# Attention of two heads at a time: rotary products on the two halves of the rows, values per tile

## The chip, the cores and the metric

The kernel runs on one core of a Trainium2 chip. The metric is the time of one execution in microseconds on the device; the median of three runs is given.

## What is computed

The reference is one layer of a diffusion backbone over 512 latent tokens and 256 context tokens, width 1024. After a modulated norm and one input projection, latent attention (4 heads) and a matrix memory (mLSTM, 4 heads) work side by side; their outputs are joined, projected and added; then a product-key retrieval of experts follows. The part that matters here is the attention. A head has 128 channels without and 64 channels with a rotary position, and reads 768 keys (256 context, 512 latent):

```
def attend(q, k, v):
    s = jnp.einsum('bhqd,bhkd->bhqk', q, k).astype(jnp.float32) * (MLA_QK ** -0.5)
    p = jax.nn.softmax(s, axis=-1).astype(v.dtype)
    return jnp.einsum('bhqk,bhkd->bhqd', p, v)
...
mla_lat, mla_ctx = mla_mixer(cols_lat[..., :MLA_COLS], ..., rope, not last)
ml_lat, ml_ctx = mlstm_mixer(cols_lat[..., MLA_COLS:], ...)
x = x + gt1 * (jnp.concatenate([mla_lat, ml_lat], axis=-1) @ w_out[l])
h2 = rmsnorm(x, g_norm2[l]) * (1.0 + sc2) + sh2
x = x + gt2 * peer(h2, w_pq[l], sub_keys[l], expert_u[l], expert_v[l])
```

Everything is float32.

## The kernel before

Tokens are cut into tiles of 128: tiles 0 to 3 are the latents. Tiles 1 to 3 go through the dense path, tile 0 goes a way of its own later on. The order of stages is: modulation and input projection; keys, values and queries; mLSTM together with the attention of tiles 1 to 3; output projection (`w_out`); the norm and the query projection of the retrieval (`w_pq`), with the sixteen best of each key half on VectorE; then `first()` and `second()`, which rank on VectorE while tile 0 is brought through and the first expert blocks are multiplied; then a long loop over 128 expert blocks (lines 1384 to 1412).

`attention(tiles, store, nm)` (line 837) is a generator. For each head and each tile it makes the scores (lines 846 and 847: for 512 and then 256 keys a product over 128 rows for the channels without position and a product over 64 rows for the rotary ones, accumulated in the same place), takes the maximum on VectorE (849), its scaled negative (850), the exponential with its sum on ScalarE (852), normalises on VectorE (853, 854), transposes the six blocks on PE (858) and copies them to `pt` on ScalarE (859). After the last tile of a head come six products with the values over all tiles of the call (864, 384 columns for three tiles), and `store` brings the result away. The queries and keys of the rotary part lie two heads in a column block: an even head on rows 0 to 63, an odd one on rows 64 to 127 (`es`). On PE each of these float32 products shows in the trace as two weight loads and two matmuls.

`split` (218, 219) writes a rounded copy on ScalarE and the rest, by subtraction, on VectorE or GpSimd. `mm3` (255 to 257) makes the three products of such pairs.

Score tiles come from a pool of two slots of 1024 columns (`wide`, tag s); from line 1029 on that pool has one slot. Results of products with the values come from a pool `jbank` of two slots, which the mLSTM steps (785, 787) use too; transposes use `bank`. `mlstm()` (736) is a generator over two pairs of heads.

`weave` draws from several generators in proportion, so that their instructions alternate in the program:

```
    weave((queries((1, 2, 3, 0)), 4), (islice(ml, CFG["w"][0]), CFG["w"][1]))
    weave((ml, CFG["w"][2]), (attention((1, 2, 3), lambda h, p_: split(ch[:, h], cl[:, h], p_), "D"), 13))
```

Tile 0 (`att0`, line 902) takes its first two steps before the norm that follows the output projection (`CFG["a"]` is (0, 2)), and the rest inside `tile0_x` (1092), after the pools have been changed. Outside the first stage and the expert loop the order on each engine is set by a planner, which takes the ready instruction that comes first in the program. `PLACE` is a list of places, one for each buffer in the order in which buffers are taken.

Of the kernel before, what the change touches and what calls it, by code (L numbers as in the profile page):

```python
# [17 lines left out]
AF = mybir.ActivationFunctionType  # L18
OP = mybir.AluOpType
AX = mybir.AxisListType  # L20
P = 128
D = 1024
# [27 lines left out]
ENDED = object()  # L50
CFG = dict(nv=2, r=8, l=(0, 34, 124), pre=28, f=(17, 7, 7, 27, 2, 4), oa=2, og=2, gt=2, a=(0, 2), ps=(('g', 2), ('j', 1), ('b', 2), ('s', 1)), w=(22, 22, 22), ko=(4, 5, 6, 7, 0, 1, 2, 3), m=(5, 7, 4, 7, 4, 4, 1), ne=lambda v, g: g, sc=lambda k, n: n == 256 or k % 2, wq=lambda nc: nc.sync, we=lambda i, v, g: g)

# [49 lines left out]
class Ring:  # L102
# [5 lines left out]
    def next(self):  # L108
        self.i += 1
        return self.v[(self.i - 1) % len(self.v)]  # L110
# [5 lines left out]
def weave(*parts):  # L116

    parts = [[g, n, 0] for g, n in parts]
    while parts:
        x = min(parts, key=lambda x: x[2] / x[1])  # L120
        x[2] += 1
        if next(x[0], ENDED) is ENDED:
            parts.remove(x)


def body(ctx, tc, nc, x_t, ctx_t, cc, w_ada_t, w_ada_n, w_in, w_uq, w_ukv, w_out, w_pq, keys_t,
         exp_u, exp_v, exp_ut, pcol, prow, pcon, rope_c, rope_s, jmat, rst, dsel, dmask, out, dbg=None):
    dbg = dbg or {}
    V, A, G, T = nc.vector, nc.scalar, nc.gpsimd, nc.tensor
# [8 lines left out]
    ar = Arena(PLACE, lambda: nc.n_instructions())  # L138
# [13 lines left out]
    start = ExitStack()  # L152
# [7 lines left out]
    def bank():  # L160
        return ps["b"].tile([P, 512], F32, name="b")

    def jbank():
        return ps["j"].tile([P, 512], F32, name="j")

    def wide():
        return ps["s"].tile([P, 1024], F32, name="s")
# [22 lines left out]
    ident = ar.take("ident", [P])  # L190
# [10 lines left out]
    small = ar.ring("small", 16, [4])  # L201
# [15 lines left out]
    def split(hi, lo, src, eng=V):  # L217
        A.activation(hi, src, AF.Copy)  # L218
        eng.tensor_tensor(lo, src, f32(hi), op=OP.subtract)  # L219
# [68 lines left out]
    with tc.manual_schedule():  # L288
# [11 lines left out]
        for j, row in enumerate((s_l, s_x)):  # L300
            for h in range(2):
                p_ = bank() if h else jbank()
# [43 lines left out]
        p_, tots = jbank(), []  # L346
# [22 lines left out]
        p_ = wide()  # L369
# [235 lines left out]
    knT, krT = ar.take("knT", [4, NT]), ar.take("krT", [2, NT])  # L605
    vm = ar.take("vm", [6, 4, P])
    knr, krpr = ar.ring("kn", 2, [4, P]), ar.ring("krp", 2, [2, 2, 64])
    for t in range(6):
        o = slice(t * P, (t + 1) * P)
        p_ = wide()  # L610
# [84 lines left out]
    def q_of(i):  # L695
        return (qn0, qr0, slice(0, P)) if i == 0 else (qnD, qrD, slice((i - 1) * P, i * P))
# [138 lines left out]
    scale = 192.0 ** -0.5  # L835

    def attention(tiles, store, nm):
        n = len(tiles) * P
        pt, ppr = ar.take("pt" + nm, [6, n]), ar.ring("pp" + nm, 2, [768])
        for h in range(4):  # L840
            es = slice((h % 2) * 64, (h % 2) * 64 + 64)
            for j, i in enumerate(tiles):
                qn, qr, o = q_of(i)
                p_ = wide()
                for c0, c1 in ((0, 512), (512, 768)):
                    T.matmul(p_[:, c0:c1], qn[:, h, o], knT[:, h, c0:c1], start=True, stop=False)  # L846
                    T.matmul(p_[:, c0:c1], qr[es, h // 2, o], krT[es, h // 2, c0:c1], start=False, stop=True)  # L847
                mx = small.next()
                V.tensor_reduce(mx[:, 0:1], p_[:, :768], axis=AX.X, op=OP.max)
                V.tensor_scalar(mx[:, 0:1], mx[:, 0:1], -scale, None, op0=OP.mult)  # L850
                pp = ppr.next()
                A.activation(pp, p_[:, :768], AF.Exp, bias=mx[:, 0:1], scale=scale, accum_out=mx[:, 1:2])
                V.reciprocal(mx[:, 1:2], mx[:, 1:2])
                V.tensor_scalar(pp, pp, mx[:, 1:2], None, op0=OP.mult)
                for t3 in range(2):
                    p_ = bank()
                    for t in range(3):
                        T.transpose(p_[:, t * P:(t + 1) * P], pp[:, (3 * t3 + t) * P:(3 * t3 + t + 1) * P], ident)
                    A.activation(pt[:, 3 * t3:3 * t3 + 3, j * P:(j + 1) * P],
                                 p_[:, :384].rearrange("p (t q) -> p t q", t=3), AF.Copy)  # L860
                if j == len(tiles) - 1:
                    p_ = jbank()[:, :n]
                    for t in range(6):
                        T.matmul(p_, vm[:, t, h], pt[:, t], start=(t == 0), stop=(t == 5))
                    store(h, p_)
                yield
        ppr.give()
        ar.give("pt" + nm)


    ch, cl = ar.take("ch", [KD, 384], F32R), ar.take("cl", [KD, 384], F32R)
    ml = mlstm()
    weave((queries((1, 2, 3, 0)), 4), (islice(ml, CFG["w"][0]), CFG["w"][1]))
    weave((ml, CFG["w"][2]), (attention((1, 2, 3), lambda h, p_: split(ch[:, h], cl[:, h], p_), "D"), 13))
    xT = ar.take("xD", [KD, 384])
    nc.sync.dma_start(xT, x_t[:, :, P:])
    for h in range(4):
        p_ = bank()
# [3 lines left out]
    p_ = bank()  # L882
# [6 lines left out]
    for wg in range(4):  # L889
        wh, wl = wpull()  # L890
        for c2 in range(2):
            k2 = 2 * wg + c2
            cs = slice(c2 * P, c2 * P + P)
            p_ = jbank()[:, :384]
# [4 lines left out]
    r2, hx = ar.take("r2", [384]), ar.ring("hx", 3, [384])  # L899

    cat0 = ar.take("cat0", [4, P])
    att0 = attention((0,), lambda h, p_: A.activation(cat0[:, h], p_, AF.Copy), "G")
    for _ in range(CFG["a"][0]):
        next(att0)
    rms_bcast(r2, hx, xT, 384)
# [2 lines left out]
    for k in range(KD):  # L908
        t = hx.next()
# [94 lines left out]
    for wg in range(8):  # L1004
# [3 lines left out]
        for c2 in range(2):  # L1008
            cs = slice(c2 * P, c2 * P + P)
            p_ = jbank()[:, :384]  # L1010
            mm3(p_, [(wh[:, k, cs], wl[:, k, cs], hi[:, k], lo[:, k]) for k in range(KD)])
            A.activation(qT[:, c2], p_, AF.Copy)
        p_ = wide()
# [408 lines left out]
    for g in range(3):  # L1422
        for half in range(2):
            d_, t = slice(half * 512, half * 512 + 512), tmr.next()
# [85 lines left out]
```

## Time and profile before

| | us |
|---|---|
| median of 3 runs | 1732.3 |
| lowest and highest | 1725.78, 1736.87 |
| profiled execution | 1736.11 |
| its span | 1734.3 |
| PE busy | 1629.1 |
| VectorE busy | 1332.7 |
| ScalarE busy | 735.3 |
| GpSimd busy | 443.6 |

The profile comes from one execution; the mean granted clock of TensorE in it is 0.975 of 2.4 GHz. PE stands for matmuls, PEld for weight loads, DVE for VectorE, ACT for ScalarE, POOL for GpSimd, SP for the queue that issues most DMAs. In a row of instructions, `s` is the score pool, `j` and `b` are the other pools of products, `sp` is on-chip memory. Start times are counted from the start of the span.

### The profile page before, as it was taken

The page shows a single profiled execution, that of the slowest core. Times are in us where ns is not written, and L with a number is a line of the kernel's source. Part 1 is how long each engine was busy: PE and PEld are TensorE (multiplying, and loading weights), DVE is VectorE, ACT ScalarE, POOL GpSimd, SP SyncE. Part 2 cuts the span into 40 slices and gives each one's busy share as a digit, 9 for nine tenths or more (in the row PEclk, how much of TensorE's full clock was granted, in tenths as well). Part 3 has the DMA queues.
Part 4 walks back from the last instruction along what each step waited for, and adds up shares of the span by engine and source line. Part 5 has one row for each costly group of instructions (what it writes and reads, how often), then busy time and mean ns, then how long its engine had stood idle before and what let it go on. Part 6 is the DMA issues. An engine that isn't in the chain of part 4 may idle for free.

```text
span 1734.3 us, 25190 instructions
## 1 busy us (share of the span) xinstructions
PE 1629.1 (94%) x9119; PEld 1412.4 (81%) x9119; DVE 1332.7 (77%) x2857; ACT 735.3 (42%) x1404; POOL 443.6 (26%) x339
## 2 busy tenths in 40 slices
PE   6889999998988999969899999999999999999988
PEld 4669854588968989857689999999999999999977
DVE  6896165556899997958876887888888888888874
ACT  4563544434345545534353433333333333334322
POOL 6621400033400000000101333333333434444311
PEclk8999988999999999989999999999999999999989
DMA  8456301133314757565777999999999999999962
GB/s 340 145 184 218 104 25 37 31 110 122 119 50 170 267 214 256 204 202 162 260 237 214 341 321 335 336 328 322 325 339 322 318 343 331 323 335 334 314 226 82
DMA packets 155244, 400.92 MB, mean 231 GB/s; under 512 B 13424, under 2 KB 70192, under 8 KB 150000
## 3 DMA queue, kind: packets, MB, share of 16 engines
q1 hardware_dynamic: 108320, 232.05, 39.0%
q0 software_dynamic: 36864, 134.23, 22.5%
q10 hardware_dynamic: 9936, 33.03, 4.9%
q8 instruction: 71, 1.16, 0.3%
q14 instruction: 53, 0.43, 0.1%
HBM read 367.28 MB, written 31.99 MB: 230 GB/s over the span
## 4 chain that ended last, share of the span: by engine, by line
PE 72%; DVE 17%; ACT 4%; DMA 4%; issue 2%; POOL 0%; ACTq 0%; SPq 0%; DVEq 0%
PE o L1283 27%; PE u L255 9%; PE u L257 9%; PE u L256 9%; PE j L255 2%; PE j L256 2%; PE j L257 2%; DVE sp L219 2%; PE s L846 1%; DVE sp L1186 1%; PE s L847 1%; PE g L1196 1%; ACT sp L218 1%; DMA sp<-in_exp_ut 1%; DMA sp<-in_w_ada_t 1%
## 5 line engine op out<-in xcount | busy, mean ns | idle before, releaser
L218 ACT ACTIVATE sp<-sp 128x512 fp32r<-128x512 f32 (+2 forms) x674 | 406.4, 637 | 465.5 <-PE u L256 257.5
L1283 PE MATMUL o<-sp 128*128 128x512 f32 x2304 | 550.1, 393 | 21.1 <-ACT sp L218 14.9
L219 DVE TENSOR_TENSOR sp<-sp,sp 128x512 fp32r<-128x512 f32 (+1 forms) x650 | 407.6, 658 | 158.7 <-ACT sp L218 158.6
L1283 PEld LDWEIGHTS o<-sp 128*128 128x128 f32 x2304 | 432.1, 189 | 113.4 <-ACT sp L218 15.8
L255 PE MATMUL u<-sp,sp 128*128 128x384 f32 x1024 | 349.2, 341 | 14.1 <-ACT sp L1269 7.8
L257 PE MATMUL u<-sp,sp 128*128 128x384 f32 x1024 | 347.8, 340 | 6.7 <-DVE sp L219 6.7
L256 PE MATMUL u<-sp,sp 128*128 128x384 f32 x1024 | 346.1, 338 | 0.0
L1347 POOL DMA_INDIRECT sp<-in_exp_u,sp x128 | 137.2, 1072 | 679.2 <-PE o L1283 360.0
L255 PEld LDWEIGHTS u<-sp,sp 128*128 128x128 f32 x1024 | 194.0, 189 | 20.9 <-ACT sp L1074 8.4
L1347 POOL DMA_INDIRECT sp<-in_exp_v,sp x128 | 151.9, 1187 | 222.3 <-DVE sp L1323 204.9
L257 PEld LDWEIGHTS u<-sp,sp 128*128 128x128 f32 x1024 | 193.7, 189 | 9.0 <-DVE sp L219 7.9
L256 PEld LDWEIGHTS u<-sp,sp 128*128 128x128 f32 x1024 | 193.8, 189 | 3.9
L219 POOL TENSOR_TENSOR sp<-sp,sp 128x2048 fp32r<-128x2048 f32 (+1 forms) x24 | 96.5, 4024 | 264.6 <-ACT sp L218 264.6
L1323 DVE SCALAR_TENSOR_TENSOR sp<-sp 128x1024 f32<-128x1024 f32 x127 | 162.5, 1279 | 0.2
L1311 DVE CUSTOM_DVE_ANT_0 sp<-sp 128x1024 f32<-128x1024 f32 x128 | 155.6, 1215 | 0.0
L257 PE MATMUL j<-sp,sp 128*128 128x256 f32 (+2 forms) x448 | 140.7, 314 | 5.0 <-DVE sp L398 5.0
L255 PE MATMUL j<-sp,sp 128*128 128x256 f32 (+2 forms) x448 | 143.0, 321 | 1.7 <-ACT sp L218 0.9
L256 PE MATMUL j<-sp,sp 128*128 128x256 f32 (+2 forms) x448 | 141.0, 315 | 0.0
L1269 ACT ACTIVATE sp<-u 128x384 f32<-128x384 f32 x100 | 49.2, 492 | 173.4 <-PE u L257 160.5
L1271 DVE TENSOR_TENSOR sp<-sp,sp 128x384 f32<-128x384 f32 x107 | 61.2, 572 | 63.2 <-ACT sp L1269 46.3
L257 PEld LDWEIGHTS j<-sp,sp 128*128 128x128 f32 x448 | 84.6, 189 | 7.5 <-DVE sp L398 5.7
L255 PEld LDWEIGHTS j<-sp,sp 128*128 128x128 f32 x448 | 84.8, 190 | 6.0 <-issue 1.7
(343 smaller groups left out, 1804.3 us busy)
## 6 DMA issues: line engine op xcount, KB each, us to landing
sp<-in_exp_ut SPq DMA_DIRECT2D x128, 512.0 KB, 5.4
sp<-in_exp_v SPq DMA_DIRECT2D x128, 512.0 KB, 6.3
gd<-sp ACTq DMA_DIRECT2D x48, 512.0 KB, 4.5
sp<-gd SPq DMA_DIRECT2D x32, 768.0 KB, 9.7
sp<-in_w_ada_t SPq DMA_DIRECT2D x38, 512.0 KB, 4.4
sp<-in_w_pq SPq DMA_DIRECT2D x16, 1024.0 KB, 5.1
sp<-in_w_in SPq DMA_DIRECT2D x8, 1024.0 KB, 5.2
sp<-in_w_out SPq DMA_DIRECT2D x8, 1024.0 KB, 4.8
```

Source lines behind the costliest of these rows:

```text
L218: A.activation(hi, src, AF.Copy)
L219: eng.tensor_tensor(lo, src, f32(hi), op=OP.subtract)
L255: T.matmul(ps, lh, rh, start=(first and i == 0), stop=False)
L256: T.matmul(ps, lh, rl, start=False, stop=False)
L257: T.matmul(ps, ll, rh, start=False, stop=(last and i == n - 1))
L846: T.matmul(p_[:, c0:c1], qn[:, h, o], knT[:, h, c0:c1], start=True, stop=False)
L1269: A.activation(ge, pu.pop(c_), AF.Gelu)
L1271: V.tensor_tensor(blk(w), blk(ge), gts[c_ // 4][:, :, c_ % 4], op=OP.mult)
L1283: T.matmul(ob[2 * g + half], l_[:, g * P:g * P + P], fl(r_), start=(c_ == 0 and i == 0), stop=(c_ == P - 1 and i == 2))
L1311: V.tensor_tensor_reduce(out=u, in0=u, in1=h2t, scale=1.0, scalar=0.0, op0=OP.mult, op1=OP.add, accum_out=act[:, j:j + 1])
L1323: V.scalar_tensor_tensor(acc, v, act[:, j:j + 1], acc, op0=OP.mult, op1=OP.add)
L1347: G.indirect_dma_start(out=r_, out_offset=None, in_=table, in_offset=bass.IndirectOffsetOnAxis(ap=col, axis=0))
```

## The change

Attention goes by pairs of heads. For each pair and each tile both heads' score tiles are taken, the two products without position are made one behind the other, then the two rotary products, of which one works on rows 0 to 63 and one on rows 64 to 127; then softmax, transposes, copies and the product with the values follow for each head, for this tile alone (128 columns). `pt` becomes a ring of two buffers of 128 columns, `store` is called for each head and tile, and the places of some buffers change. The number of steps that the generator gives to `weave` stays.

```
-        n = len(tiles) * P
-        pt, ppr = ar.take("pt" + nm, [6, n]), ar.ring("pp" + nm, 2, [768])
-        for h in range(4):
-            es = slice((h % 2) * 64, (h % 2) * 64 + 64)
+        ptr, ppr = ar.ring("pt" + nm, 2, [6, P]), ar.ring("pp" + nm, 2, [768])
+        for pair in range(2):
             for j, i in enumerate(tiles):
                 qn, qr, o = q_of(i)
-                p_ = wide()
+                S = [wide(), wide()]
                 for c0, c1 in ((0, 512), (512, 768)):
-                    T.matmul(p_[:, c0:c1], qn[:, h, o], knT[:, h, c0:c1], start=True, stop=False)
-                    T.matmul(p_[:, c0:c1], qr[es, h // 2, o], krT[es, h // 2, c0:c1], start=False, stop=True)
+                    for e in range(2):
+                        T.matmul(S[e][:, c0:c1], qn[:, 2 * pair + e, o], knT[:, 2 * pair + e, c0:c1], start=True, stop=False)
+                    for e in range(2):
+                        es = slice(e * 64, e * 64 + 64)
+                        T.matmul(S[e][:, c0:c1], qr[es, pair, o], krT[es, pair, c0:c1], start=False, stop=True)
...
+                for e in range(2):
+                    h, p_, mx = 2 * pair + e, S[e], small.next()
...
+                    pp, pt = ppr.next(), ptr.next()
...
+                        A.activation(pt[:, 3 * t3:3 * t3 + 3], p_[:, :384].rearrange("p (t q) -> p t q", t=3), AF.Copy)
+                    p_ = jbank()[:, :P]
                     for t in range(6):
                         T.matmul(p_, vm[:, t, h], pt[:, t], start=(t == 0), stop=(t == 5))
-                    store(h, p_)
-                yield
+                    store(h, j, p_)
+                    yield
...
-    weave((ml, CFG["w"][2]), (attention((1, 2, 3), lambda h, p_: split(ch[:, h], cl[:, h], p_), "D"), 13))
+    weave((ml, CFG["w"][2]), (attention((1, 2, 3), lambda h, j, p_: split(ch[:, h, j * P:j * P + P], cl[:, h, j * P:j * P + P], p_), "D"), 13))
```

## Rows read from the trace of the kernel before

**Rows 1.** The page: busy us of each engine, share of the span, instructions.
```profile
PE 1629.1 (94%) x9119; PEld 1412.4 (81%) x9119; DVE 1332.7 (77%) x2857; ACT 735.3 (42%) x1404; POOL 443.6 (26%) x339
```
**Rows 2.** Table of stretches: length, busy us by engine, granted clock, DMA, GB/s.
```profile
285.00:300.00 15.00, 14.97 (x78) 8.86 (x76) 5.83 (x17) 5.22 (x13) 0.00 (x0) 1.00 0.00 0
...
315.00:330.00 15.00, 15.00 (x61) 7.46 (x60) 9.48 (x21) 5.73 (x14) 0.00 (x0) 1.00 0.04 10
...
440.00:500.00 60.00, 53.77 (x304) 49.78 (x302) 57.62 (x346) 16.89 (x26) 13.75 (x3) 0.97 0.29 93
...
900.00:1734.00 834.00, 819.35 (x4124) 745.10 (x4122) 657.34 (x987) 315.94 (x590) 285.76 (x251) 0.99 0.87 304
```
**Rows 3.** Timeline, 250 to 300 us: start, us, engine, line, idle time before.
```profile
260.00 0.70 PE L847 MATMUL s<-sp,sp 64*128 64x256 f32 x2
...
261.51 0.95 DVE L849 TENSOR_REDUCE sp<-s 128x1 f32<-128x768 f32 x1
...
266.33 2.07 PE L846 MATMUL s<-sp,sp 128*128 128x512 f32 x2 [0.86 <-ACT sp L852]
```
**Rows 4.** Table of stretches of 5 us after the first scores.
```profile
260.00:265.00 5.00, 1.82 (x10) 1.25 (x10) 5.00 (x10) 2.54 (x4) 2.00 (x4) 0.96 0.59 210
265.00:270.00 5.00, 4.14 (x7) 1.07 (x5) 4.27 (x7) 3.44 (x11) 1.02 (x2) 0.50 0.16 41
...
275.00:280.00 5.00, 5.00 (x15) 2.69 (x16) 2.97 (x8) 3.59 (x10) 0.00 (x0) 0.67 0.00 0
```
**Rows 5.** Chain of waits in order of time, 200 to 360 us.
```profile
300.03 1.05 PE s L846 x2
301.09 1.05 PE s L847 x2
302.14 0.63 PE s L846 x2
302.77 0.63 PE s L847 x2
...
304.45 0.66 PE b L858 x6
305.11 1.05 PE s L847 x2
...
352.05 0.43 PE s L846 x2
352.49 0.53 PE j L255 x2
```
**Rows 6.** The same chain: products with the values of one head.
```profile
306.16 4.07 PE j L864 x12
```
**Rows 7.** Timeline of PE, 319.6 to 321.2 us.
```profile
319.72 0.69 PE L847 MATMUL s<-sp,sp 64*128 64x512 f32 x1
319.80 0.49 PE L785 MATMUL j<-sp,sp 64*128 64x129 f32 x2
320.25 0.59 PE L847 MATMUL s<-sp,sp 64*128 64x512 f32 x1
320.77 0.70 PE L846 MATMUL s<-sp,sp 128*128 128x256 f32 x2
```
**Rows 8.** Chain of waits, 352 to 560 us: tile 0's output projection.
```profile
525.29 2.05 PE j L1101 x16
...
533.86 1.78 PE j L1101 x16
```
**Rows 9.** Groups by line and shape, 185 to 345 us: busy us, mean ns, idle before.
```profile
L789 ACT ACTIVATE sp<-j,sp 128x129 f32<-128x129 f32 x32 | 11.8, 368 | 18.9 <-PE j L785 13.4 <-PE s L847 4.2 <-DVE sp L804 0.8
...
L218 ACT ACTIVATE sp<-j 128x384 fp32r<-128x384 f32 x3 | 1.5, 487 | 7.0 <-PE j L864 7.0
```
**Rows 10.** Timeline, 300 to 355 us: softmax of one score tile.
```profile
300.07 0.96 DVE L849 TENSOR_REDUCE sp<-s 128x1 f32<-128x768 f32 x1 [0.24 <-PE s L847]
...
301.38 0.90 ACT L852 ACTIVATE sp<-s,sp 128x768 f32<-128x768 f32 x1 [2.30 <-DVE sp L850]
```

More of the change, by code (lines that the diff above doesn't have):

```diff
@@ L837, in attention @@
     def attention(tiles, store, nm):
-        n = len(tiles) * P
-        pt, ppr = ar.take("pt" + nm, [6, n]), ar.ring("pp" + nm, 2, [768])
-        for h in range(4):
-            es = slice((h % 2) * 64, (h % 2) * 64 + 64)
+        ptr, ppr = ar.ring("pt" + nm, 2, [6, P]), ar.ring("pp" + nm, 2, [768])
+        for pair in range(2):
             for j, i in enumerate(tiles):
                 qn, qr, o = q_of(i)
-                p_ = wide()
+                S = [wide(), wide()]
                 for c0, c1 in ((0, 512), (512, 768)):
-                    T.matmul(p_[:, c0:c1], qn[:, h, o], knT[:, h, c0:c1], start=True, stop=False)
-                    T.matmul(p_[:, c0:c1], qr[es, h // 2, o], krT[es, h // 2, c0:c1], start=False, stop=True)
[L848 to L862, printed above, removed]
@@ new lines, in attention @@
+                    for e in range(2):
[5 more added lines that the diff above has]
+                    h, p_, mx = 2 * pair + e, S[e], small.next()
+                    V.tensor_reduce(mx[:, 0:1], p_[:, :768], axis=AX.X, op=OP.max)
+                    V.tensor_scalar(mx[:, 0:1], mx[:, 0:1], -scale, None, op0=OP.mult)
+                    pp, pt = ppr.next(), ptr.next()
+                    A.activation(pp, p_[:, :768], AF.Exp, bias=mx[:, 0:1], scale=scale, accum_out=mx[:, 1:2])
+                    V.reciprocal(mx[:, 1:2], mx[:, 1:2])
+                    V.tensor_scalar(pp, pp, mx[:, 1:2], None, op0=OP.mult)
+                    for t3 in range(2):
+                        p_ = bank()
+                        for t in range(3):
+                            T.transpose(p_[:, t * P:(t + 1) * P], pp[:, (3 * t3 + t) * P:(3 * t3 + t + 1) * P], ident)
+                        A.activation(pt[:, 3 * t3:3 * t3 + 3], p_[:, :384].rearrange("p (t q) -> p t q", t=3), AF.Copy)
+                    p_ = jbank()[:, :P]
@@ L863, in attention @@
                     for t in range(6):
                         T.matmul(p_, vm[:, t, h], pt[:, t], start=(t == 0), stop=(t == 5))
-                    store(h, p_)
-                yield
+                    store(h, j, p_)
+                    yield
         ppr.give()
-        ar.give("pt" + nm)
+        ptr.give()
     ch, cl = ar.take("ch", [KD, 384], F32R), ar.take("cl", [KD, 384], F32R)
@@ L901, in body @@
     cat0 = ar.take("cat0", [4, P])
-    att0 = attention((0,), lambda h, p_: A.activation(cat0[:, h], p_, AF.Copy), "G")
+    att0 = attention((0,), lambda h, j, p_: A.activation(cat0[:, h], p_, AF.Copy), "G")
     for _ in range(CFG["a"][0]):
```

20 rows, old and new, of the table PLACE are left out of this document.

## Prediction

> **What bounds the kernel now.** I went from the whole to the place. The page's busy times first: TensorE is busy for 94% of the span and no other engine comes near it [rows 1]. A mean over stages says little about one stage, so the table of stretches comes next: in the stage where attention runs beside the mLSTM part, PE is busy 14.97 to 15.00 of every 15 us, while VectorE and ScalarE are at 5 to 10 [rows 2]. What this stage saves on PE should therefore come out at its end, and nothing else is late there. Further on VectorE is the full engine for a while (57.62 of 60 us), and after that PE again (819 of 834 us) [rows 2]. VectorE's stretch begins with the scores that PE hands it, so an earlier PE moves it forward as a whole; I see nothing between 353 us and the end that would start at a fixed time of its own.
>
> There is one hole in the stage. The scores of the first two head-tiles are done at 260.7 us, VectorE comes to the first maximum only at 261.51, and PE gets its next score product at 266.33, when the first slot of the score pool is released by the exponential [rows 3]. In that hole PE is busy 1.82 of 5 us, and the granted clock afterwards is 0.50 of 2.4 GHz, that is 1.2 GHz, until about 278 us [rows 4].
>
> **The change part by part.** *What a score costs today.* In the chain of waits at full clock the no-rotary product over 512 keys takes 1.05 us, the rotary one 1.05, over 256 keys 0.63 and 0.63: 3.36 us for a head and a tile, 6.72 for two heads [rows 5]. Each product is two instructions. Twelve instructions of 384 columns in a row take 4.07 us, 0.339 each or 0.883 ns a column [rows 6]; at that pace 512 columns twice are 0.90 us and 256 twice 0.45. So about 0.15 to 0.18 us of each score product is the price of changing between a product over 128 rows and one over 64.
>
> *Two no-rotary products in a row* change the shape once, not twice: 1.05 + 0.90 and 0.63 + 0.45, so 0.15 + 0.18 = 0.33 us less for two heads.
>
> *Two rotary products on the two halves of the rows.* The trace has the nearest thing by accident: a rotary product of 512 keys (L847) with an mLSTM product of 64 rows (L785, two passes of 129) started inside it. The L847 couple begins at 319.72, the next product over 128 rows at 320.77: 1.05 us, what it takes alone, and the L785 couple keeps its usual 0.49 [rows 7]. So the second half of the rows came free. If the second head's rotary product comes free in the same way, two heads save 1.05 + 0.63 = 1.68 us; if it does not run alongside, they save 0. The row is for 129 columns beside 512, so that 512 beside 512 is free is my reading and not shown.
>
> That row also bears on a rule of the Trainium skill, "TensorE: Matmul & The Clock Gate", Part 3 (packing small matmuls): matmuls start and end in program order without exception. By it the first pass of the second head could start only with the second pass of the first, and a packed couple would take three passes instead of two. In the row both passes of L785 start before the second pass of L847 (319.80 against 320.25), but the row does not tell which of the two was issued first, so it leaves the rule open; the rule's time is a rival below.
>
> Together: 0.33 + 1.68 = **2.01 us for two heads and a tile**. Tiles 1 to 3 have six such pairs. The first lies ahead of the hole, where PE waits for VectorE anyway: nothing. Tile 0's first pair was run inside the full stage by the planner as filling (the last of its score products stand at 352 us, just ahead of the first projection [rows 5]) and counts. The second pair of tile 0 runs after the score pool has shrunk to one slot: its second tile can only be written when the first has been released, so its products stay apart as today, at no gain and no loss. Six pairs count: 12.1 us if all stay together.
>
> *How many stay together.* The order on PE is not the program's: the planner puts in whatever is ready. Of the 24 couples of no-rotary and rotary product of tiles 1 to 3 I count 13 with nothing between them and 11 with transposes, mLSTM products or a product with the values in between, like the six transposes at 304.45 [rows 5]. Besides, the two slots are released one after the other (below), so that the first head's rotary product is often ready before the second head's slot is free, and would be issued alone. I take half: 6.0 us. Both ends stay for the range: 0 and 12.1.
>
> *Product with the values per tile.* Today 12 instructions of 384 columns, 4.07 us a head [rows 6]; afterwards 36 of 128 columns. The nearest row is the plain product of 128 columns for tile 0, 16 instructions in 1.78 to 2.05 us, 0.111 to 0.128 each [rows 8]: 4.0 to 4.6 us a head, so from 0.3 us less to 2.2 more over four heads. I take 0.111, since that row was at full clock inside a run of its kind: no change. It starts three times as often, each time behind an eviction of transposes. Eight starts more, at nothing if other work stands in front, at about the 0.2 us of a change of shape if not: 0 to 1.6 us. I take 0.5.
>
> *Evictions of the results.* Four of 384 columns become twelve of 128: ScalarE 12 x 0.37 - 4 x 0.49 = +2.5 us [rows 9]; VectorE makes as many subtractions of the same width, for which I put the same again at most. Beside ScalarE's 5.7 and VectorE's 9.5 busy us of 15 [rows 2] that is hidden; without that cover it is 5 us. The projections that follow read the mLSTM half of the channels first, so the last eviction has time.
>
> *The wait that is added.* A pair takes both slots of the score pool. From the end of a score the maximum (0.96 us), its scaling and the exponential (0.90) release a slot after about 2.2 us, 300.07 to 302.28 [rows 10]; the second slot follows about one maximum later, at 3.2. Today PE fills one slot while the other is read. Afterwards the next pair's first product waits 2.2 us, and what is queued behind it on PE in the planned order waits too; mLSTM products, and the transposes and value products of the pair before, can stand in front of it. Some 18 us of mLSTM work are spread over the stage (82 us from 270 to 352, less 12 x (3.36 + 0.66) + 4 x 4.07 = 64.5 of attention [rows 5, 6]), 3 us for each pair, so I take 1 us in all, for the last pairs, when mLSTM is over. Bounds: 0 and 11 (five pairs at 2.2). The product with the values also asks the two-slot pool that the mLSTM steps use twelve times instead of four, but for a third as long each time: 0. The lines that change issue no DMA and use no queue of SP or POOL. The moved buffers may meet a former tenant's last reader: no row prices it; 0, with 3 us to either side in the range.
>
> **Sum:** -6.0 + 0.5 + 1.0 = -4.5 us. Against the profiled execution (1736.11 us, of which the span is 1734.3) that is 1731.6. The median of the three runs shown is 1732.3, 3.8 under the profiled one, so the forecast for the median is **1728 us**. A measurement of this kernel can tell about 1% (17 us) from no change, and even the full gain is less.
>
> **Rivals.** *All pairs hold* (the planner finds both slots free because PE is behind anyway, as its full stretches suggest): 12.1 less 0.5, and less nothing for slots, gives 1721. Against it: 11 of 24 couples are broken today. *Strict order of passes:* the rotary couple takes 1.05 + 0.43 and 0.63 + 0.21 us, saves 1.04 instead of 1.68, and half of 6 x 1.37 less 1.5 is 2.6 us: 1730. *It doesn't do what it says* (the planner separates nearly all the rotary couples, or 512 beside 512 doesn't overlap): 6 x 0.33 less 1.5 is nothing, 1732. *Slower by the slots:* each pair drains PE for 2.2 us because nothing is ready in front, 5 x 2.2 = 11 us, against 6 saved; and a longer gap brings the low clock back once more, as after 260.7 us, where about 10 us at half clock [rows 4] did 5 us of work: +10, 1742. It decides from the point where PE's idle time between 280 and 350 us passes about 5 us; today, from 285 to 330, it is 0.03 us [rows 2]. For it: the slots are taken in pairs without exception; against it: PE has a backlog there.
>
> **Chances.** Forecast case (half of the couples) 0.45, all pairs hold 0.18, strict order 0.10, not what it says 0.12, slower by the slots 0.15. The cases reach from 1721 to 1742; with the 5 us by which single runs scatter, and 3 for the placement, the range that leaves out 2 in 10 is 1716 to 1741. Faster by over 1% (under 1715) needs the full gain and luck further on: 0.05. Slower by over 1% (over 1750) needs several falls of the clock: 0.05. Within 1%: 0.90.
>
> **What would show it.** Two rotary products of 512 keys starting within 0.1 us of each other, and done about 1.05 us after the first, show the overlap; three passes in length show strict order. The count of couples kept shows the factor of a half. Idle time of PE ahead of the no-rotary product, ended by the exponential, prices the slots; a granted clock of 0.50 anywhere from 280 to 350 us shows the slower rival. The first projection over the output weights should start some 4 us earlier than 352.5 [rows 5]. I am wrong if it starts earlier and the end doesn't move: then something between (VectorE's stretch) has slack that I didn't see.

## The result and the profile after

The changed kernel takes 1762.24 us (median of 4 runs, 1758.59 to 1765.76) beside 1733.59 for the kernel before in the same session: a ratio of 1.0165, 95% interval 1.0133 to 1.0198. It is slower by some 29 us. The forecast was 1728 us, and 1762 lies outside its range. The profiled execution took 1762.02 us, its span 1760.2, 25.9 more than before's.

The page's first line (busy us, share, instructions) hardly moved against [rows 1]; PE, the bound, is busy 10.7 us more, which does not make 25.9.

```profile
PE 1639.8 (93%) x9215; PEld 1429.9 (81%) x9215; DVE 1327.4 (75%) x2865; ACT 738.2 (42%) x1412; POOL 444.5 (25%) x339
```

The table of stretches tells where the rest is. I cut out the stage from the first score product to the weight load of the first transpose of `hs`, just ahead of the output projection. Columns as in [rows 2]: length, busy us of PE, PEld, DVE, ACT and POOL, granted clock, DMA. Before:

```profile
253.70:350.90 97.20, 92.17 (x350) 47.85 (x350) 54.77 (x109) 43.85 (x99) 7.09 (x5) 0.93 0.10 30
```

After, the same stage, then the stretches that answer to [rows 2] and two of 5 us inside:

```profile
251.30:367.00 115.70, 101.32 (x441) 61.65 (x440) 50.30 (x113) 45.22 (x105) 9.39 (x6) 0.82 0.07 21
285.00:300.00 15.00, 11.95 (x49) 7.56 (x50) 4.84 (x12) 3.87 (x9) 0.00 (x0) 0.78 0.00 0
290.00:295.00 5.00, 1.95 (x7) 0.83 (x7) 2.92 (x8) 1.88 (x4) 0.00 (x0) 0.84 0.00 0
295.00:300.00 5.00, 5.00 (x15) 3.20 (x14) 0.76 (x2) 0.98 (x2) 0.00 (x0) 0.50 0.00 0
315.00:330.00 15.00, 11.95 (x55) 7.96 (x54) 4.64 (x11) 4.75 (x11) 0.00 (x0) 0.77 0.00 0
```

The stage is 18.5 us longer. PE, which had 14.97 of 15 us before [rows 2], now has 11.95, and no other engine is full in its place. Behind such a hole (1.95 busy of 5 us) the granted clock is 0.50, that is 1.2 GHz. The trace's clock record has 13.7 us at 0.50 in the stage before (those of [rows 4]) and 41.0 after, in five pieces: one of 10.2 us near the start, as before, and four that begin inside the four waits counted below, 0.3 to 1.2 us before each ends. With these the stage adds up. Of the time at 0.50 PE was busy 12.8 us before and 37.7 after (it idled in the rest), and I count half of that as the price of the low clock. Work at full clock (busy less that half) goes from 85.8 to 82.5, of which 2.3 is only moved (one rotary product of 512 keys and one couple of 256 stand behind the cut now): some 1 us saved. Idle time goes from 5.0 to 14.4, +9.4. The low clock costs 6.4 before and 18.8 after, +12.5. Together -3.3 + 9.4 + 12.5 = 18.6. This is an estimate from one execution of each kernel.

The waits of PE from 255 to 405 us name the idle time (us in total, times, longest):

```profile
PE s L846 <- ACT sp L855: 12.8, 4, 3.5
```

Before, that wait had 1.5 us in two pieces. One hole in the timeline, to be read beside [rows 3, 10]:

```profile
289.40 1.03 PE L846 MATMUL s<-sp,sp 128*128 128x256 f32 x4
...
290.36 0.70 PE L849 MATMUL s<-sp,sp 64*128 64x256 f32 x4
291.09 1.82 DVE L852 TENSOR_REDUCE sp<-s 128x1 f32<-128x768 f32 x2 [0.99 <-PE s L849]
292.83 0.27 DVE L853 TENSOR_SCALAR sp<-sp 128x1 f32<-128x1 f32 x2
293.07 0.90 ACT L855 ACTIVATE sp<-s,sp 128x768 f32<-128x768 f32 x1 [3.52 <-DVE sp L853]
...
293.96 0.89 ACT L855 ACTIVATE sp<-s,sp 128x768 f32<-128x768 f32 x1
...
294.12 2.07 PE L846 MATMUL s<-sp,sp 128*128 128x512 f32 x2 [3.05 <-ACT sp L855]
```

Both heads' scores end together at 291.06. VectorE then takes both maxima (x2, 1.82 us) and only afterwards both scalings, so the first exponential starts at 293.07, not 1.3 us after its maximum began as in [rows 10]; the first slot is free at 294.0, PE has idled 3.05 us, and its next product takes 2.07 us instead of 1.12. The transposes of this pair need the same softmax, and those of the pair before are done. Whether mLSTM work was ready is not shown: the next such product (L785) starts at 301.01 without a wait of its own, behind the waiting score product in TensorE's order.

The chain of waits after, the lines that answer to [rows 5, 6, 7]:

```profile
280.24 1.34 PE j L865 x12
...
290.43 0.68 PE s L849 x4
...
310.14 1.05 PE s L849 x2
...
312.44 1.05 PE s L849 x2
313.50 1.06 PE s L846 x4
314.56 0.68 PE s L849 x4
...
369.49 0.18 PE j L255
```

Two rotary products of 256 keys together take 0.68 us, where one took 0.63: the overlap is there. The two of 512 keys, here at 310.14 and 312.44, went separately in every pair, each at 1.05 where the clock was full. Twelve instructions with the values are 1.34 to 1.54 us at full clock, three times that 4.0 to 4.6 against 4.07 [rows 6]. The first projection starts at 369.49, not at 352.49 [rows 5].

Behind the stage I measure from there to the point where TensorE's queue reaches the first product with the experts' output weights and begins to wait for it (L1284 after, 768.3 us; the product itself starts at 781.7, before at 756.7). This distance is 401.3 us, before 391.9: another 9.4. As the stage began 2.3 us earlier, 18.5 + 9.4 - 2.3 makes the 25.9 of the span, within 0.3.

### The profile page after: what moved, and what is told of

Read it like the earlier page. It is cut to its first block, busy times and chain, and to the rows that moved or that the text cites. A ratio compares the mean times of both kernels' runs of the same rounds, so it can differ in the third digit from the quotient of the medians.

```text
span 1760.2 us, 25409 instructions
## 1 busy us (share of the span) xinstructions
PE 1639.8 (93%) x9215; PEld 1429.9 (81%) x9215; DVE 1327.4 (75%) x2865; ACT 738.2 (42%) x1412; POOL 444.5 (25%) x339
## 4 chain that ended last, share of the span: by engine, by line
PE 72%; DVE 15%; DMA 4%; ACT 3%; issue 2%; POOL 0%; ACTq 0%; SPq 0%; DVEq 0%
PE o L1284 27%; PE u L255 9%; PE u L257 9%; PE u L256 9%; PE j L255 2%; PE j L256 2%; PE j L257 2%; DVE sp L219 2%; PE s L846 2%; DVE sp L1187 1%; DMA sp<-in_w_ada_t 1%; PE j L865 1%; PE s L849 1%; PE g L1197 1%; ACT sp L218 1%
## 5 line engine op out<-in xcount | busy, mean ns | idle before, releaser
L1284 PE MATMUL o<-sp 128*128 128x512 f32 x2304 | 551.6, 394 | 20.4 <-ACT sp L218 13.5
L1284 PEld LDWEIGHTS o<-sp 128*128 128x128 f32 x2304 | 433.7, 189 | 112.7 <-ACT sp L218 14.5
```

Source lines behind the costliest of these rows:

```text
L1284: T.matmul(ob[2 * g + half], l_[:, g * P:g * P + P], fl(r_), start=(c_ == 0 and i == 0), stop=(c_ == P - 1 and i == 2))
```

## The experiments

Theory after the trace: making both heads' scores side by side empties PE for a whole softmax, and the clock falls after it. Rivals: the value products per tile cost the time, tile 0 does, or the moved places. Ratios are to the kernel before on the same chip, with 95% intervals; "low clock" is the time at 0.50 in the stage; "rest" is the distance behind the stage as above. Lengths are from the profiled execution alone, which can lie some us off the median: that of e9 took 1741.25 us, that of e14 1729.64. The kernel before had a median of 1733.59 to 1737.39 us beside the different runs, so rows are compared by their ratios.

| kernel | median us | ratio | stage us | low clock us | rest us |
|---|---|---|---|---|---|
| before | 1733.59 | | 97.2 | 13.7 | 391.9 |
| after | 1762.24 | 1.0165 [1.0133, 1.0198] | 115.7 | 41.0 | 401.3 |
| e1 values per tile only | 1744.75 | 1.0056 [1.0035, 1.0077] | 105.8 | 20.5 | 393.5 |
| e2 head after head | 1736.88 | 1.0021 [1.0003, 1.0039] | 98.3 | 13.7 | 395.5 |
| e3 filled holes | 1755.40 | 1.0119 [1.0098, 1.0141] | 110.8 | 13.7 | 403.2 |
| e4 values late | 1748.95 | 1.0091 [1.0065, 1.0116] | 106.9 | 34.1 | 398.5 |
| e5 tile 0 only | 1737.83 | 0.9995 [0.9970, 1.0019] | 97.1 | 13.7 | 393.9 |
| e6 tiles 1 to 3 only | 1764.76 | 1.0165 [1.0113, 1.0218] | 114.5 | 34.1 | 404.1 |
| e7 late from the second pair | 1747.05 | 1.0054 [1.0037, 1.0071] | 102.2 | 23.9 | 400.1 |
| e8 scaling on GpSimd | 1741.73 | 1.0026 [1.0005, 1.0048] | 99.5 | 6.8 | 392.5 |
| e9 = e7 + e8 | 1736.28 | 0.9999 [0.9981, 1.0016] | 89.2 | 3.4 | 405.8 |
| e10 = e2 + e8 | 1734.58 | 0.9977 [0.9963, 0.9991] | 93.6 | 3.4 | 393.9 |
| e11 before + e8 | 1736.41 | 1.0004 [0.9984, 1.0023] | 91.1 | 6.8 | 399.2 |
| e12 before, spill late | 1742.13 | 1.0027 [1.0012, 1.0043] | 97.0 | 13.7 | 401.4 |
| e13 after, spill early | 1757.55 | 1.0145 [1.0112, 1.0177] | 115.1 | 34.1 | 397.8 |
| e14 = e9, spill early | 1734.94 | 1.0003 [0.9984, 1.0021] | 87.5 | 0.0 | 399.8 |
| e15 = e11, spill early | 1734.26 | 0.9994 [0.9977, 1.0010] | 90.7 | 3.4 | 399.5 |

### Which part of the change costs

**e1, values per tile only.** The changed kernel with scores head by head as before; transposes and product with the values per tile as after, in the places of after.

```
-        for pair in range(2):
+        for h in range(4):
...
-                S = [wide(), wide()]
+                p_ = wide()
...
+                    T.matmul(p_[:, c0:c1], qn[:, h, o], knT[:, h, c0:c1], start=True, stop=False)
+                    T.matmul(p_[:, c0:c1], qr[es, h // 2, o], krT[es, h // 2, c0:c1], start=False, stop=True)
```

> The scores go head after head as in the kernel before, each head-tile takes one slot; only the product with the values per tile, its two small buffers, the evictions by tile and the new places stay. Theory of the slots (both slots of the score pool end together, TensorE waits about 3 us for the exponential four times, and the clock falls after each wait): the holes are gone, about 1734 us, within 5 of the kernel before. Theory of the values (more starts, more weight loads and evictions, the pool shared with the mLSTM steps): the loss stays, 1755 or more. If the 10 us that are lost after the stage come from the new places, about 1743.

Ratio 1.0056: a loss of its own. The median lies near the 1743 that was expected if the new places cost the time behind the stage, but not for that reason: the rest grew by 1.6 us, the stage by 8.6. In the stage there is one new hole. In the timeline of e1:

```profile
334.06 0.70 PE L847 MATMUL s<-sp,sp 64*128 64x256 f32 x2
...
335.26 1.28 ACT L821 ACT_TABLE_LOAD   x1
...
336.88 1.28 ACT L852 ACT_TABLE_LOAD   x1
...
338.17 0.90 ACT L852 ACTIVATE sp<-s,sp 128x768 f32<-128x768 f32 x1
...
339.22 2.07 PE L846 MATMUL s<-sp,sp 128*128 128x512 f32 x2 [4.46 <-ACT sp L852]
```

Here VectorE and ScalarE are busy with the end of mLSTM and the softmax comes late; twice 1.28 us of it ScalarE loads a function table, for mLSTM's root and then for the exponential. At the same place before, with the same two loads, the long product with the values of a whole head covers it (timeline of before):

```profile
331.59 4.14 PE L864 MATMUL j<-sp 128*128 128x384 f32 x12 [0.25 <-ACT sp L859]
336.41 1.12 PE L846 MATMUL s<-sp,sp 128*128 128x512 f32 x2 [0.68 <-ACT sp L852]
```

So that product was cover there, and cut into three it no longer stands there. That this alone makes the ratio is read from the two timelines; no run isolates it.

**e2, head after head.** The pair, its two slots and the values per tile stay; the four score products of the first head come before those of the second.

```
-                for c0, c1 in ((0, 512), (512, 768)):
-                    for e in range(2):
+                for e in range(2):
+                    es = slice(e * 64, e * 64 + 64)
+                    for c0, c1 in ((0, 512), (512, 768)):
```

> As the changed kernel, with both slots taken for a pair, but the program makes all four products of the first head and then all four of the second, so the first head's softmax can begin some 3 us before the second head's scores end. Theory of the slots: it is the common end of both heads that opens the hole; with staggered ends the next pair's first product finds its slot free about when it is wanted, 1735 to 1745 us. If taking two slots at once is enough for the hole: still 1755 to 1765. Theory of the values: 1760.

Ratio 1.0021, low clock as before, stage 98.3. Of the loss of 1.65% all but 0.2 goes with the order of the products. It is not the taking of two slots by itself, nor the moved places, which e2 has too: it is that the first score is finished no earlier than the second. The stage of e2, to be read beside that of after:

```profile
254.10:352.40 98.30, 92.79 (x443) 56.43 (x443) 56.01 (x115) 44.62 (x106) 8.64 (x6) 0.93 0.07 25
```

**e5 and e6, tile 0 only, and tiles 1 to 3 only.** Two generators, each used for one of the calls.

```
-    weave((ml, CFG["w"][2]), (attention((1, 2, 3), lambda h, p_: split(ch[:, h], cl[:, h], p_), "D"), 13))
+    weave((ml, CFG["w"][2]), (pairs((1, 2, 3), lambda h, j, p_: split(ch[:, h, j * P:j * P + P], cl[:, h, j * P:j * P + P], p_), "D"), 13))
...
-    att0 = attention((0,), lambda h, p_: A.activation(cat0[:, h], p_, AF.Copy), "G")
+    att0 = pairs((0,), lambda h, j, p_: A.activation(cat0[:, h], p_, AF.Copy), "G")
```

Against the kernel before, e5 has the second of these edits alone, e6 the first alone, each with some moved places.

> Tiles 1 to 3 keep the attention of the kernel before; only tile 0 goes by pairs with the values per tile (three buffers beside it find other places). Of the 26 us some 9 are lost after the first projection. If these come from the pairs of tile 0 itself (its score products no longer fill gaps of the stage before, and its other work is displaced into full stretches): 1739 to 1744 us. If they only follow from the shift of everything behind the first stage: 1733 to 1736.

> The other half: tiles 1 to 3 by pairs as in the changed kernel, tile 0 as in the kernel before. Theory of the slots: the holes of the first stage stay, with some 17 us of loss: 1750 to 1754 us if the loss further on belongs to tile 0, 1758 to 1762 if it belongs to the shift. If tile 0 were the main cause: 1740.

0.9995 and 1.0165: the whole loss lies with tiles 1 to 3. The growth behind the stage comes with them too (rest 404.1), so it does not need tile 0's own pairs; by the ratio e6 lies where it was expected in that case.

### Hole and clock

**e3, filled holes.** The changed kernel with 24 transposes of the identity behind each pair's scores in tiles 1 to 3, work that nobody reads.

```
+                if len(tiles) > 1:
+                    d_ = bank()
+                    for t in range(24):
+                        T.transpose(d_[:, t % 4 * P:t % 4 * P + P], ident, ident)
```

> As the changed kernel, with 24 transposes of a constant (about 2.6 us at full clock) behind the scores of each pair of tiles 1 to 3; nothing reads them. If about half of the loss is the half clock after each hole (some 27 us more at 0.50 in the stage than before, so some 13 us of work): the transposes lie in the holes, the clock stays at 1.00, and the time falls to 1748 to 1754 though work was added. If the holes cost only their own length: no change, 1760 to 1765. If PE was not waiting at all in most pairs: 16 us more, 1775.

It is 144 instructions longer, some 16 us at 0.111 [rows 8], and 0.46% faster than the changed kernel (1.0119 against 1.0165; the intervals just overlap), somewhat less than was expected. Where the holes were, the table of stretches of e3 has:

```profile
290.00:295.00 5.00, 5.00 (x35) 3.52 (x34) 1.28 (x6) 1.51 (x4) 0.00 (x0) 1.00 0.00 0
315.00:320.00 5.00, 5.00 (x28) 3.05 (x27) 1.61 (x5) 1.39 (x4) 0.00 (x0) 1.00 0.00 0
```

Full and at full clock; the time at 0.50 in the stage falls from 41.0 to 13.7 us. So the low clock is the hole's consequence, and filling the hole with waste was no worse than leaving it, by the medians better.

**e4, values late.** Transposes, copies and products with the values of a pair are emitted behind the next pair's scores, as useful filling.

```
+                if len(tiles) > 1:
+                    while late:
+                        values(*late.pop(0))
...
+                    late.append((h, j, pp))
```

> As the changed kernel (pairs, rotary products side by side, values per tile), but the transposes and the product with the values of a pair stand in the program behind the scores of the next pair, so that PE has 4 us of work while the softmax frees the slots. Theory of the slots: the holes close and the saving in the rotary products shows, 1722 to 1738 us. Theory of the values: nothing of it is removed, 1755 to 1765. If the loss after the stage (10 of 26 us) is a matter of its own, it stays: 1735 to 1745.

Nearly half of the loss goes (1.0091), a time between those expected. The holes are 4.3 us in three pieces, but the low clock is still 34.1 us, 23.9 of it from 260.8 us on, where the first pair's transposes and products have been moved away. The run also shows the disputed overlap. In its timeline all four passes of two rotary products over 512 keys stand together:

```profile
290.26 1.13 PE L863 MATMUL s<-sp,sp 64*128 64x512 f32 x4
291.32 1.13 PE L860 MATMUL s<-sp,sp 128*128 128x256 f32 x4
```

Four passes take 1.13 us (1.06 in the chain), what two take alone (1.12 and 1.05); the first two start within 0.01 us of each other, and so do the last two. The Trainium skill ("TensorE: Matmul & The Clock Gate", Part 3) says that matmuls start and end in program order. If both passes of the first product were issued ahead of those of the second, that order would take the time of three passes, and the trace, with the time of two, does not agree. The trace does not show the order of issue: with the passes of the two products issued in turn, rule and row agree.

**e7, late from the second pair.** As e4, but the first pair keeps its own transposes and products.

```
-                    if len(tiles) == 1:
+                    if len(tiles) == 1 or (pair, j) == (0, 0):
```

> As the run with late values, but the first pair's transposes and values stand directly behind its softmax, where the planner could use them as filling between 262 and 285 us. In the run with late values the clock was at half for 23.9 us there, against 13.7 in the kernel before; if that came from putting the first values off, the time falls by about 5 us to 1744; if the mLSTM chain sets it, it stays at 1749.

1.0054, against 1.0091 of e4 (the intervals just overlap), some 6 us as was expected if putting the first values off did the harm. The low clock at the start is back to before's 13.7 us; 10.2 remain behind one hole of 3.0 us at the end of mLSTM, at 333 us.

**e8, scaling on GpSimd.** The changed kernel; VectorE keeps the maxima and loses the two scalings that stood behind both of them.

```
-                    V.tensor_scalar(mx[:, 0:1], mx[:, 0:1], -scale, None, op0=OP.mult)
+                    G.tensor_scalar(mx[:, 0:1], mx[:, 0:1], -scale, None, op0=OP.mult)
```

> As the changed kernel, with the scaled negative of the maximum made on GpSimd, which is idle in this stage, in place of VectorE. On VectorE both maxima came ahead of the first scaling, so the first exponential waited for the second head's maximum too, 0.95 us in each of four holes. If the length of the hole is what counts: the holes shrink from 3.1 to 2.2 or 2.5 us and the time falls by 3 us, by up to 10 where the clock then no longer falls: 1752 to 1759. If the wait for the slots is not in the maximum: no change, 1762.

1.0026: by the ratios one line brings back some 24 us, far more than the 3 to 10 that were expected. Timeline of e8:

```profile
314.27 1.82 DVE L852 TENSOR_REDUCE sp<-s 128x1 f32<-128x768 f32 x2 [2.24 <-PE s L849]
315.32 0.21 POOL L853 TENSOR_SCALAR sp<-sp 128x1 f32<-128x1 f32 x1 [20.88 <-DVE sp L852]
315.56 0.90 ACT L855 ACTIVATE sp<-s,sp 128x768 f32<-128x768 f32 x1 [4.07 <-POOL sp L853]
...
316.61 1.12 PE L846 MATMUL s<-sp,sp 128*128 128x512 f32 x2 [2.36 <-ACT sp L855]
```

The exponential starts 1.3 us after the first maximum, not 2.0; the hole is 2.36 us, and the product behind it runs at full clock. Of three holes of 2.4 us in e8 one was followed by the low clock; the four of after (3.05 to 3.50) all were. The stage is 16.2 us shorter, and nearly all of that is the clock: its price falls from 18.8 to 3.2 us. The four holes fall from 12.8 to 8.3 us, but idle time as a whole only from 14.4 to 12.7, since other waits are back, of which 3.2 us for GpSimd (L764) stand in the kernel before too. The rest is 8.8 us shorter as well, which the edit does not touch directly.

### Where the rest went

Combinations of these mends, to find whether the saving can be had without the hole.

**e9, e10 and e11.** The edit of e8 on e7 (e9), on e2 (e10) and on the kernel before (e11).

```
-                    V.tensor_scalar(mx[:, 0:1], mx[:, 0:1], -scale, None, op0=OP.mult)
+                    G.tensor_scalar(mx[:, 0:1], mx[:, 0:1], -scale, None, op0=OP.mult)
```

> Pairs with late values from the second pair on, and the scaling on GpSimd: both remedies of the wait in one kernel. If each removes what the other leaves (the holes closed by work, the first and the last wait shortened so that the clock stays), the saving of the rotary products shows: 1725 to 1732 us. If the two remove the same wait: 1740 to 1747, as each alone.

> The run with head after head in the pair, with the scaling on GpSimd. Its only hole left is the one ahead of 264 us, which brings 13.7 us at half clock; the scaling waits there behind other work of VectorE. If that wait shortens the clock's fall as it did in the run with pairs (6.8 in place of 13.7 us): 1729 to 1734 us. If not: 1737.

> The kernel before with nothing changed but the scaling on GpSimd. If what hurts is how long TensorE waits for the first exponential: the fall of the clock at 264 us is shortened from 13.7 to about 7 us and 3 to 4 us are gained, 1731 to 1735 against 1737 now. If the scaling matters only where both maxima stand together: no change.

e9's stage is 89.2 us, 8 shorter than before's, and e11's 91.1, but both end with before (0.9999 and 1.0004), slower than was hoped: their rest is 405.8 and 399.2 us. e10 keeps its smaller gain; 0.9977 is the only interval under 1 among fifteen kernels, and the best that was found, 0.2%.

**e12, spill late.** One thing differs in the rest of after, e9 and e11 from that of before, e2, e8 and e10: the 24 transposes that spill tiles 1 to 3 all lie behind the first key score, in the full stretch of the query projections, instead of all ahead of it. e12 does that to the kernel before, by ordering them behind the score product of the same round.

```
-                T.matmul(p_[:, (2 * j + c2) * P:(2 * j + c2 + 1) * P], qT[:, c2, j * P:(j + 1) * P],
+                last = T.matmul(p_[:, (2 * j + c2) * P:(2 * j + c2 + 1) * P], qT[:, c2, j * P:(j + 1) * P],
...
-            spill(wg, lambda k: xT[:, k, (wg - 1) * P:wg * P], xtr)
+            with tc.issue_after(last.ins):
+                spill(wg, lambda k: xT[:, k, (wg - 1) * P:wg * P], xtr)
```

> The kernel before with one order edge more: the 24 transposes that bring tiles 1 to 3 back to rows are issued behind the score product of the same round of the query projection, where they lie in all the kernels that lost some 9 us after the first projection; no work is added. If this displacement is the cause of that loss: 4 us (24 transposes and their change of stage in a full stretch) up to 9 us more, 1741 to 1746. If it only goes along with it: within 2 us of the kernel before.

1.0027, some 4.7 us, as expected. The groups by line from 412 to 484.9 us in the kernel before, where the last four transposes end just ahead of the first key score at 413.74, and in the stretch of the key scores after (count, busy us, mean ns):

```profile
L922 PE MATMUL b<-sp 128*128 128x128 f32 x4 | 0.6, 272 | 0.0
```

```profile
L923 PE MATMUL b<-sp 128*128 128x128 f32 x24 | 3.1, 272 | 0.0
```

From its first to its last product the stretch of the key scores is 71.2 us before, 74.6 after and 74.0 in e12. In all the traces it is 71.1 to 71.2 with the transposes ahead of it and 74.0 to 74.6 with them inside.

**e13, e14 and e15, spill early.** The same transposes ahead of the loop of query projections in the program: on after, e9 and e11.

```
+    for t in range(1, 4):
+        spill(t, lambda k: xT[:, k, (t - 1) * P:t * P], xtr)
...
-        if 1 <= wg <= 3:
-            spill(wg, lambda k: xT[:, k, (wg - 1) * P:wg * P], xtr)
```

> The changed kernel with one step moved in the program: the 24 transposes that spill tiles 1 to 3 are emitted ahead of the loop of query projections, so that they can't come to lie inside its full stretch. Theory (the some 9 us that the changed kernel loses behind its first projection are in part these displaced transposes: putting them there cost the kernel before 4.7 us): 1753 to 1758, and the time from the first transpose of hs to the first product of the gates falls from 401 to some 396. Rival (they cost nothing where they lie in the changed kernel, the loss has another place): 1760 to 1764.

> Both mends of the wait (the late transposes from the second pair on, the scaling on GpSimd) with the spill of tiles 1 to 3 emitted early. Theory (the mended stage ends some 9 us earlier, and only the displaced transposes gave it back): 1726 to 1731. Rival (what follows the stage runs to dates of its own and takes back whatever the stage saves): 1735 to 1738.

> The kernel before with the scaling on GpSimd and the spill of tiles 1 to 3 emitted early. Theory of the displaced transposes: 1728 to 1733, its stage having been some 9 us shorter than that of the kernel before. Rival (what follows runs to dates of its own): 1735 to 1738.

e13 comes out where the theory put it, at 1757.55 and a rest of 397.8, but its interval overlaps that of after, its low clock in the stage was 6.8 us shorter, and the gain is not where the theory had it: the stretch of the key scores is 3.4 us shorter (71.2), but from the norm's sum (L268) to the first key score it is 2.7 longer (23.0 against 20.3). So e13 shows no price. e14 and e15 miss. e14's stage has no low clock at all:

```profile
250.40:337.90 87.50, 83.08 (x440) 52.62 (x440) 48.68 (x101) 46.61 (x107) 12.13 (x18) 1.00 0.08 28
```

That is 9.7 us shorter than before's, and its median is before's (1.0003). The profiled execution, one of its fastest, was 6.5 us faster than before's, so how much of the saving the others lose, and where, one trace does not show. In it the stretch of the key scores is back at 71.1 us, but from the norm's sum to the first key score, where the transposes lie now, it takes 22.9 us against 19.1 before, and the rest is 399.8. The transposes did not come back into idle time, and the three runs do not isolate their price.

## Why the prediction was wrong

**The step that failed** is "the wait that is added": "so I take 1 us in all, for the last pairs, when mLSTM is over. Bounds: 0 and 11". It was 12.8 us in four holes, above the upper bound, and two of the four lay inside the mLSTM stage, a third at its end; behind them the clock fell, for which the forecast has no term: +12.5 us. Two reasons. First, I let mLSTM products and the previous pair's transposes "stand in front", and at the four holes nothing stood there. They came at 291, 315, 336 and 355 us, where the last products of both heads stand together and the next instruction in TensorE's order is the next pair's first product, which waits for the slot. Second, the length: I took 2.2 us from [rows 10], one head's softmax. With two scores ready at once VectorE does maximum, maximum, scaling, scaling, and 2.2 becomes 3.05. e8 takes out just that order and brings some 24 us, mostly by the clock.

**The rival "slower by the slots"** named the mechanism, the place and the sign to look for (0.50 between 280 and 350 us), and its point of decision, about 5 us of idle time, was passed. It was mis-sized: five drains of 2.2 us were 11, measured 12.8 in four; one more fall of the clock was 5 us (10 us at half clock), measured +12.5 in the stage from several; 6 us were to be saved, some 1 was; and the growth behind the stage, 9.4, is not in it. I gave it 0.15 for PE's backlog, and the backlog was what the change took away: the full stretches of [rows 2] were full because one head's scores stood beside the other head's softmax, as they do again in e2. The hole from which it was priced was also read too simply: of the idle time from 260.7 to 266.33 us only 0.86 us waited for the exponential [rows 3], and 3.18 us for GpSimd, for mLSTM (timeline of before):

```profile
263.88 0.65 PE L769 MATMUL b<-sp,sp 128*128 128x128 f32 x4 [3.18 <-POOL sp L764]
```

The chance of 0.05 for slower by over 1% belonged to "several falls of the clock", which is what came.

**Overlap of the rotary products:** right. 512 beside 512 is free (1.06 us, e4), 256 beside 256 takes 0.68.

**Half of the couples:** wrong in kind. Of the six couples of 256 keys of tiles 1 to 3 four stayed together, those at 290.36, 314.49, 335.12 and 352.83 us, and of the six of 512 none. The prediction feared that the first head's rotary product would go alone because its slot comes free earlier. That parts the products without position (294.12 and 297.26), but in that pair the rotary ones came only at 310.07 and 312.38, with mLSTM products between them: why the planner put them there is not shown. Four times about 0.6 us is 2.3, not 6; of it some 1 us shows in the work of the stage.

**Product with the values per tile:** its own time was right (4.0 to 4.6 us a head). Its "eight starts more" at 0.5 missed what the timelines of e1 and before show, that the long product was cover: one hole of 4.5 us and a fall of the clock, in a kernel that is some 10 us slower.

**Evictions:** 12 x 0.278 = 3.3 us on ScalarE against 4 x 0.487 = 2.0 [rows 9], hidden as said; I had taken 2.5 more, it is 1.3.

```profile
L218 ACT ACTIVATE sp<-j 128x128 fp32r<-128x128 f32 x12 | 3.3, 278 | 22.7 <-PE j L865 22.7
```

**"I see nothing between 353 us and the end that would start at a fixed time":** a delay of the stage was not carried one to one, it grew by 9.4 us, and a stage shorter by 8 to 10 us (e9, e14) brought nothing in the median. By place: 3.4 us in the stretch of the key scores, where the displaced transposes are 3.1 us of work, 1.2 ahead of it, where they are missing and nothing got shorter, 2.7 from tile 0's projection to the query projection of its norm, 2.6 from the gates to the end of the distance. e12 prices the displacement at 4.7 us in the kernel before. By kind, the two distances:

```profile
350.90:742.80 391.90, 363.66 (x2691) 338.66 (x2689) 336.62 (x1071) 187.83 (x354) 47.41 (x11) 0.98 0.48 168
```

```profile
367.00:768.30 401.30, 369.78 (x2698) 343.67 (x2697) 339.17 (x1075) 189.11 (x357) 45.91 (x10) 0.97 0.47 165
```

The clock is in it here too: 13.7 us at 0.50 before, 23.9 after. Counted as for the stage, the low clock makes 5.0 of the 9.4 us, idle time 3.3, work 1.1. Every kernel with a rest of over 397 us has 23.9 us or more at 0.50 in it (e9 37.5), every one under 396 has 20.5 or less. What makes the clock fall more often there is not settled; that tile 0's first scores, filling in the stage before, come partly behind it now is a candidate that no run isolated.

## What to carry to other kernels

Two accumulators that are drained by the same two engines give overlap only while one is filled as the other is read: a change that fills both together has to be costed as one whole drain per pair, with both drains' instructions in the order in which the reading engine will take them. A full engine is no proof of a backlog: ask which instruction covers each wait today, and whether the change cuts that one up. Where the clock falls after a hole, price the hole at more than its length; here the low clock cost 12.5 us more beside 9.4 of idle time, and e8, whose holes are 1.2 to 2.4 us instead of 3.05 to 3.50, got back 15.7 us of the clock's price and only 1.7 of idle time.

## What the hardware showed unexpectedly

Two float32 products on rows 0 to 63 and 64 to 127 run side by side in both their passes, four passes of 512 columns in 1.06 to 1.13 us.

The length of a hole alone does not tell whether the clock falls. In after, 3.05 us was followed by 0.50 at 294.12 and at 318.24; in e13 a hole of the same length was followed by a product at full clock (timeline of e13, 1.12 us, not 2.07):

```profile
297.71 1.12 PE L846 MATMUL s<-sp,sp 128*128 128x512 f32 x2 [3.05 <-ACT sp L855]
```

Its holes of 3.15 and 3.50 us were followed by 2.08 and 2.07 again. What decides between them these runs do not show.
